# Rotating the banded attention's tensors in halves, with shorter pauses, in a two-layer hybrid backbone kernel

## The chip, the cores and the metric

The kernel runs on one core of one Trainium2 chip. The metric is the device time of one execution in microseconds, taken as the median of several runs. The engines are TensorE (PE; its weight loads are PEld), VectorE (DVE), ScalarE (ACT), GpSimd (POOL) and SyncE (SP), which issues nearly all DMA transfers.

## What is computed

The reference is a backbone of two layers over 1024 latent tokens and 256 context tokens, 1024 wide, in f32. Each layer splits one input projection among three kinds of heads, concatenates what they give, projects it back, and ends with a gated MLP:

```python
qa, kva, kr, z, xbc, dtr, swq, swk, swv = split_cols(h @ p['w_in'], IN_SPLITS)
...
qa_l = mla_queries(qa, p['mla_q_norm_g'], p['mla_w_uq'], pos)      # rotated by position
y_a = mla_latent_attention(qa_l, ka, va, ka_c, va_c)               # A: 6 heads, dense
...
yb, _ = ssd_bidirectional(xs, bm, cm, dt, a, h_ctx, True)          # B: scan, both directions
y_b = ssd_output(yb, xs, z, p['ssm_d'], p['ssm_norm_g'])
...
qs = axial_rope(swq.reshape(b, s, SWA_HEADS, SWA_HEAD_DIM), *pos) * scale
ks = axial_rope(swk.reshape(b, s, SWA_KV_HEADS, SWA_HEAD_DIM), *pos)
y_c = swa_latent_attention(qs, ks, vs, ks_c, vs_c, p['swa_sink'])  # C: banded, 4 heads
x = x + g1 * (jnp.concatenate([y_a, y_b, y_c], axis=-1) @ p['w_out'])
x = x + g2 * conv_glu(h2, p['ffn_w_up'], p['ffn_conv_w'], p['ffn_conv_b'], p['ffn_w_down'])
```

`axial_rope` is the rotation that the change is about: each tensor is multiplied by a cosine table, a copy of it with pairs exchanged is multiplied by a sine table, and the two are added. The first layer updates the context tokens too, the second does not.

## The kernel before

Tokens lie along the free axis, channels along the partitions, so a row tile is 128 x 1280 (1024 latent columns, then 256 context columns; `LAT` and `CTXS` in the code). A product in full precision is three matmuls on a high and a low part of each operand (`qh`, `ql`, `kh`, `kl`; `mixh`, `mixl`; `wh`, `wl`): the high part is a ScalarE copy to fp32r, the low part a VectorE subtraction.

In the middle of each layer the dense latent attention (A) is the foreground. Head after head it walks over ten key tiles; for each there are scores (`s<-qh,kh` and its two low products), an exponential on ScalarE (L1442), an addition to the sum of exponentials (`acc`, L1449, on GpSimd or VectorE), and matmuls with the values (`py<-P,vt`). The maxima of the next head (`pm`, `px`, reduced on VectorE at L1358 and L1349, then `mr` L1364 and the transposition `pr`) are made meanwhile.

In the background of that, one generator, `side()`, runs first the scan (B, function `ssd`), then the banded attention (C, function `swa`). The foreground keeps a modelled time, `self.t`, which only its and the background's matmuls advance. At each of its calls of `tick()` the background is let go one step further if the time that it asked for has come; a `yield p` asks for a pause of `p` modelled microseconds. The pauses stand in the table `PACE`, with one number for each layer. So the text of the program, and with it the order on TensorE, is set when the kernel is written out. On ScalarE and VectorE a background instruction is held behind the foreground instruction that was written ahead of it.

The last steps of the scan's generator are, for each chunk, the outputs (`main`), the pause `sq`, and `tail`: the sum of squares `py<-ones,z` on TensorE, whose input z is an ACT product (L998) behind VectorE's L994 and L996. Then `swa` begins. It loads its tensors from DRAM (`swr`, L1046), rotates the keys and the two halves of the queries one after the other (`rotate`, L788 to L793: shuffle, times sine, times cosine, addition, each 128 x 1024), splits them (copy L1049, subtraction L1050), writes both parts to DRAM (L1052) and pauses for `rot`. After the pause `sw0` come its own maxima (`sx`, `sb`, `sr`) and then units of work: scores `s<-qq,kk`, exponentials, additions to `acc` (L1176 to L1179), values, and at the end `pd`, a reciprocal (L1195) and the product `yc` (L1196). The first layer has six units, the second four.

When `swa` is done, its pool is closed, a new pool is opened in that memory, and the first two weights of the output projection (`w_out`) are loaded into it (`wload`, L413; split by L423 and L424). Another stage reads `w_out`'s other operand, `mixh` and `mixl`, the split of the concatenated heads (L798, L799). The projection's first matmuls are `p<-mixh,w`.

Of the kernel before, what the change touches and what calls it, by code (L numbers as in the profile page):

```python
# [20 lines left out]
SEQ = 1024  # L21
# [26 lines left out]
CTXS = slice(SEQ, NT)  # L48
# [11 lines left out]
def _rope_tables():  # L60
# [23 lines left out]
PACE = {  # L84
    'dt': (22.0, 22.0),
    'back0': (4.0, 4.0),
    'back': (3.0, 3.0),
    'cb': (0.5, 0.5),
    'exp': (0.5, 0.5),
    'ce': (0.5, 0.5),  # L90
    'fwd0': (4.0, 4.0),
    'fwd1': (5.0, 5.0),
    'sq': (2.0, 2.0),
    'next': (1.5, 1.5),
    'rot': (3.0, 3.0),
    'sw0': (14.0, 14.0),
    'swm0': (1.0, 1.0),
    'swa': (1.0, 1.0),
    'swb': (1.0, 1.0),
    'swv': (1.0, 1.0),  # L100
    'swx': (1.0, 1.0),
    'swe': (6.0, 6.0),
    'qpe': (6.0, 6.0),
    'mx1': (1.5, 1.5),
    'mx2': (1.5, 1.5),
    'mx3': (1.5, 1.5),
# [8 lines left out]
class Emit:  # L115
# [672 lines left out]
    def rotate(self, t, sh, cos, sin, rows, mask):  # L788
# [3 lines left out]
        nc.vector.tensor_mul(t[:rows, LAT], t[:rows, LAT], cos[:rows, LAT])  # L792
        nc.vector.tensor_add(t[:rows, LAT], t[:rows, LAT], sh[:rows, LAT])  # L793

    def split(self, src, rows, n, name, pool=False):
        nc = self.nc
        h, lo = self.u(F32R, name=name + "h"), self.u(F32R, name=name + "l")
        nc.scalar.copy(h[:rows, :n], src[:rows, :n])  # L798
        (nc.gpsimd if pool else nc.vector).tensor_sub(lo[:rows, :n], src[:rows, :n], h[:rows, :n])  # L799
        return h, lo  # L800


    def ssd(self, l, krdt, out):
        nc, c = self.nc, l == 0
# [87 lines left out]
        order = [9, 8] + list(range(7, 0, -1))  # L892
# [16 lines left out]
        order = [8, 9] + list(range(8))  # L909
        st = {}  # L910

        def load(k):
            s = st[k] = {"tm": load_tm(k)}
            if not (c or k < 8):
                return
            s["fm"] = M.tile([128, 7, 128], F32, tag="fm", name=self.nm("fm"))
            nc.sync.dma_start(out=s["fm"], in_=self.fmd[k])
            s["ab"] = []
            for d in range(2):
                ab = M.tile([128, SH, 128], F32, tag="ab", name=self.nm("ab"))  # L920
                nc.sync.dma_start(out=ab, in_=self.acsd[d * 6:d * 6 + 6, k, :].unsqueeze(0).to_broadcast([128, SH, 128]))
                s["ab"].append(ab)
            s["hb"] = None
            if k != 9:
                s["hb"] = M.tile([128, 384], F32, tag="hb", name=self.nm("hb"))
                nc.sync.dma_start(out=s["hb"], in_=self.hbd[k])
            s["z"] = M.tile([128, 3, 128], F32, tag="z", name=self.nm("z"))
            nc.sync.dma_start(out=s["z"], in_=self.zd[k])
# [72 lines left out]
        def tail(k):  # L1001

            s = st.pop(k)
            if "py" not in s:
                return
            for i in range(3):
                self.mm(out=s["py"][:, 384:385], lhsT=s["z"][:, i, :], rhs=self.ones[:, 0:1], start=(i == 0), stop=(i == 2))
            nc.vector.tensor_copy(vst[:, k:k + 1], s["py"][:, 384:385])
# [9 lines left out]
        for i, k in enumerate(order):  # L1018
            hf = main(k, hf)
            if i + 1 < len(order):  # L1020
                yield from prep(order[i + 1])
            yield PACE['sq'][l]
            tail(k)
            if i + 2 < len(order):
                load(order[i + 2])
            yield PACE['next'][l]
        n = NCH if c else 8
# [4 lines left out]
    def swa(self, l, Y):  # L1032
        nc, c = self.nc, l == 0
        sm = self.small[l]
        mask = [i ^ 16 for i in range(32)]
# [4 lines left out]
        cos, sin = self.u(name="cos"), self.u(name="sin")  # L1040
        nc.sync.dma_start(out=cos[:, LAT], in_=self.I['rope'][2])
        nc.sync.dma_start(out=sin[:, LAT], in_=self.I['rope'][3])
        for i in (0, 2, 3):
            n = NT if i == 0 else nq
            t, sh = self.u(name="swr"), self.u(name="sh")
            nc.sync.dma_start(out=t[:, 0:n], in_=self.swd[i][:, 0:n])  # L1046
            self.rotate(t, sh, cos, sin, 128, mask)
            h = [M.tile([128, NT], F32R, tag="k", name=self.nm(x)) for x in ("swh", "swl")]
            nc.scalar.copy(h[0][:, 0:n], t[:, 0:n])  # L1049
            nc.vector.tensor_sub(h[1][:, 0:n], t[:, 0:n], h[0][:, 0:n])  # L1050
            for p in range(2):
                nc.sync.dma_start(out=self.shd[i][p][:, 0:n], in_=h[p][:, 0:n].bitcast(F32))  # L1052
            yield PACE['rot'][l]
        vr, vt = self.u(name="swv"), self.u(name="vt")
        nc.sync.dma_start(out=vr, in_=self.swd[1])
        yc = [self.u(name="yc") for _ in range(2)]
# [71 lines left out]
        for u, (kv, s0, e0) in enumerate(units):  # L1128
# [19 lines left out]
            for i, (k, c0, c1) in enumerate(todo):  # L1148
                n = c1 - c0
# [51 lines left out]
    def mla_proj(self, l, kva, qn, kbuf, qh, load, maxes):  # L1201

        nc, c = self.nc, l == 0
# [20 lines left out]

        def rotated(t):

            self.rotate(t, self.u(name="sh"), cos, sin, 128, mask)
            yield PACE['qpe'][l]
            qp = self.split(t, 128, nq, "qp")
            for p in range(2):  # L1230
                nc.sync.dma_start(out=self.qpd[1][p][:, 0:nq], in_=qp[p][:, 0:nq].bitcast(F32))
# [37 lines left out]
        mask = [i ^ 8 for i in range(32)]  # L1269
        cos, sin = self.u(name="cos"), self.u(name="sin")  # L1270
# [29 lines left out]
        t = self.u(name="qpe")  # L1300
        small(wq, qn, 448, 128, some, self.evac(t, 128))
        self.bg(rotated(t), 1.0)
        values(range(2, 4))
        key(1)
# [932 lines left out]
```

## Time and profile before

| what | value |
|---|---|
| median of three runs | 3254.55 us (3251.92 to 3255.03) |
| the profiled execution | 3257.76 us |
| its span in the trace | 3255.6 us |
| granted TensorE clock, mean over the span | 0.965 |
| TensorE busy | 3057.9 us, 94% |
| VectorE busy | 2126.9 us, 65% |
| ScalarE busy | 1273.0 us, 39% |
| attention stage, first layer | about 400 to 788 us |
| attention stage, second layer | about 2080 to 2458 us |

The clock is given as a share of full speed. Its two levels are 1.2 and 2.4 GHz, so that a stretch with a mean of 0.65 was partly at the lower one. A wait of TensorE counts directly, as it is busy for 94% of the span; waits of the other engines count only where TensorE waits for them.

### The profile page before, as it was taken

What the parts mean: (1) busy time and instruction counts of PE and PEld (TensorE: products, weight loads), DVE (VectorE), ACT (ScalarE), POOL (GpSimd) and SP (SyncE); (2) the same over time, 40 slices, a digit from 0 to 9 for tenths busy, and PEclk for the clock granted to TensorE, in tenths of its full rate; (3) what the DMA queues carried; (4) which work ended last, traced back from release to release, by engine and by line L of the source; (5) the groups of instructions that cost most, each with busy time, mean ns of one, the idle gap of its engine ahead of it and who ended that gap; (6) DMA issues with size and microseconds to landing.
All of it is one profiled execution on the core that took longest, in us unless ns stands there. A gap on an engine that the chain in (4) does not pass through costs nothing.

```text
span 3255.6 us, 40074 instructions
## 1 busy us (share of the span) xinstructions
PE 3057.9 (94%) x15369; PEld 2404.6 (74%) x15369; DVE 2126.9 (65%) x3250; ACT 1273.0 (39%) x2204; POOL 421.0 (13%) x259
## 2 busy tenths in 40 slices
PE   6989978998999999998999999888999999999998
PEld 4778754554878888887888788754557778888887
DVE  4785787776285566668865635887563667677544
ACT  5334543443263343343111543543342444444212
POOL 2101113543100000000001200123452000000001
PEclk8999988999999999999999999988999999999999
DMA  8665676102312212227543345754113122225321
GB/s 269 217 194 152 215 223 168 39 16 86 106 41 67 78 56 72 78 67 287 179 149 104 122 112 169 236 168 131 42 35 115 52 78 80 89 84 180 131 75 62
DMA packets 349247, 392.41 MB, mean 121 GB/s; under 512 B 37202, under 2 KB 276451, under 8 KB 349056
## 3 DMA queue, kind: packets, MB, share of 16 engines
q1 hardware_dynamic: 348092, 389.62, 37.9%
q8 instruction: 121, 1.98, 0.3%
q0 software_dynamic: 704, 0.14, 0.1%
q14 instruction: 70, 0.57, 0.1%
q10 hardware_dynamic: 260, 0.10, 0.0%
HBM read 284.48 MB, written 104.01 MB: 119 GB/s over the span
## 4 chain that ended last, share of the span: by engine, by line
PE 80%; DVE 13%; ACT 2%; issue 2%; DMA 2%; POOL 0%; SPq 0%; DVEq 0%; ACTq 0%; POOLq 0%
PE p L143 36%; PE X L143 10%; PE Z L143 7%; PE s L143 5%; PE py L143 5%; PE pc L143 4%; PE V L143 3%; PE Y L143 3%; DVE mx L1358 1%; PE pm L143 1%; PE pn L143 1%; DVE wm L354 1%; PE pst L143 1%; DMA xr<-in_x_dram 1%; DVE acc L1393 1%
## 5 line engine op out<-in xcount | busy, mean ns | idle before, releaser
L143 PE MATMUL p<-gh,wb 128*128 128x512 f32 (+1 forms) x1760 | 504.9, 371 | 0.0
L436 ACT CAST wb<-w 128x512 fp32r<-128x512 f32 (+1 forms) x412 | 251.5, 613 | 597.4 <-PE p L143 304.4
L437 DVE TENSOR_TENSOR wb<-w,wb 128x512 fp32r<-128x512 f32 (+1 forms) x412 | 279.1, 679 | 239.4 <-ACT wb L436 237.9
L143 PEld LDWEIGHTS p<-gh,wb 128*128 128x128 f32 x1760 | 321.1, 189 | 56.0 <-issue 0.2
L1568 DVE SCALAR_TENSOR_TENSOR x<-p,modT,x 128x512 f32<-128x512 f32 (+1 forms) x280 | 193.0, 694 | 249.2 <-PE p L143 248.8
L143 PE MATMUL X<-hb,wb 128*128 128x512 f32 x1440 | 340.4, 389 | 1.6 <-DVE cm L1606 1.6
L143 PE MATMUL p<-gl,wb 128*128 128x512 f32 (+1 forms) x880 | 325.3, 370 | 0.3 <-DVE gl L1747 0.3
L143 PEld LDWEIGHTS X<-hb,wb 128*128 128x128 f32 x1440 | 270.1, 188 | 58.5 <-DVE cm L1606 2.5
L143 PE MATMUL p<-hhi,wh 128*128 128x512 f32 (+1 forms) x792 | 292.7, 377 | 5.5 <-ACT z L643 3.3
L143 PE MATMUL p<-hlo,wh 128*128 128x512 f32 (+3 forms) x792 | 290.8, 368 | 1.4 <-POOL hlo L2139 0.9
L143 PE MATMUL p<-hhi,wl 128*128 128x512 f32 (+1 forms) x744 | 272.7, 367 | 2.3 <-DVE wl L424 2.3
L1442 ACT ACTIVATE P<-s 128x512 f32<-128x512 f32 x240 | 142.3, 598 | 240.7 <-PE s L143 236.0
L143 PE MATMUL Z<-hb,wb 128*128 128x512 f32 x960 | 233.0, 392 | 3.6 <-ACT cm L1608 3.6
L143 PEld LDWEIGHTS Z<-hb,wb 128*128 128x128 f32 x960 | 179.9, 189 | 41.1 <-ACT cm L1608 4.4
L1449 POOL TENSOR_TENSOR acc<-acc,P 128x1024 f32<-128x1024 f32 x69 | 168.7, 2446 | 234.4 <-ACT P L1442 200.8
L143 PEld LDWEIGHTS p<-gl,wb 128*128 128x128 f32 x880 | 166.8, 190 | 28.4 <-DVE gl L1747 0.8
L143 PEld LDWEIGHTS p<-hhi,wh 128*128 128x128 f32 x792 | 152.6, 194 | 34.6 <-issue 4.4
L143 PE MATMUL py<-P,vt 128*64 128x512 f32 (+3 forms) x744 | 175.5, 588 | 0.2 <-DVE mx L1358 0.2
L143 PEld LDWEIGHTS p<-hlo,wh 128*128 128x128 f32 (+1 forms) x792 | 150.3, 190 | 24.6 <-DVE hlo L2133 1.5
L2085 POOL TENSOR_TENSOR acc<-acc,sq 128x512 f32<-128x512 f32 x24 | 32.0, 1339 | 1021.4 <-ACT sq L2084 1021.4
L143 PEld LDWEIGHTS p<-hhi,wl 128*128 128x128 f32 x744 | 142.8, 192 | 26.4 <-DVE wl L424 3.2
L354 DVE SCALAR_TENSOR_TENSOR wm<-wm,mstat,wm 128x512 f32<-128x512 f32 x196 | 141.1, 745 | 23.4 <-DMA wm<-in_w_mod_dram 22.8
(404 smaller groups left out, 5794.8 us busy)
## 6 DMA issues: line engine op xcount, KB each, us to landing
wm<-in_w_mod_dram SPq DMA_DIRECT2D x96, 512.0 KB
w<-in_ffn_w_up_dram SPq DMA_DIRECT2D x88, 512.0 KB
w<-in_ffn_w_down_dram SPq DMA_DIRECT2D x32, 512.0 KB
w<-in_w_in_dram SPq DMA_DIRECT2D x30, 512.0 KB
gd<-ft SPq DMA_DIRECT2D x22, 640.0 KB
gr<-gd SPq DMA_DIRECT2D x22, 640.0 KB
ab<-acsd SPq DMA_DIRECT2D x36, 384.0 KB
tm<-tmd SPq DMA_DIRECT2D x38, 320.0 KB
```

The source lines that it names most:

```text
L143: self.nc.tensor.matmul(out=out, lhsT=lhsT, rhs=rhs, start=start, stop=stop, **kw)
L354: nc.vector.scalar_tensor_tensor(out=acc[:, v, :], in0=w[:, i, :], scalar=c, in1=acc[:, v, :], op0=ALU.mult, op1=ALU.add)
L436: self.nc.scalar.copy(t[:, 0], raw)
L437: self.nc.vector.tensor_sub(t[:, 1], raw, t[:, 0])
L1358: nc.vector.tensor_reduce(out=m[:, j, s:s + 1], in_=p, axis=AXX, op=ALU.max)
L1393: nc.vector.reciprocal(rc, pd)
L1442: nc.scalar.activation(P[:, q * 512:(q + 1) * 512], s, AF.Exp, scale=sc)
L1449: (nc.vector if kt in ((2, 4, 6, 8) if self.scan else (4, 7)) else nc.gpsimd).tensor_add(acc, acc, P)
L1568: self.nc.vector.scalar_tensor_tensor(out=t[:, s:e], in0=p[:, 0:e - s], scalar=self.mcol(l, v, m)[:, o:o + 1], in1=t[:, s:e], op0=ALU.mult ...
L2085: (nc.gpsimd if self.n[ch] < 6 else nc.vector).tensor_add(acc, acc, sq[:, :n])
```

## The change

The three rotations in `swa` go by halves of 512 columns, and each operation is a step of the generator of its own, with a pause of 0.7 behind it (1.4 behind the addition and the copy); the subtraction of a half follows that pause. The 256 context columns are split in a step of their own. The rotation of the latent queries in `mla_proj` goes by halves too, with two pauses of 0.7 in each. `sw0` falls from 14 to 10 and `qpe` from 6 to 4. The pause `sq` of the last chunk of the scan grows by 4.

```diff
-    'rot': (3.0, 3.0),
-    'sw0': (14.0, 14.0),
+    'rot': (0.7, 0.7),
+    'sw0': (10.0, 10.0),
...
-    'qpe': (6.0, 6.0),
+    'qpe': (4.0, 4.0),
...
+    def rotate_steps(self, t, sh, cos, sin, rows, mask, hi, lo, n, pause):
+
+        nc, v = self.nc, self.nc.vector
+        for a in (0, 512):
+            r = slice(a, a + 512)
+            v.stream_shuffle(sh[rows, r], t[rows, r], mask)
+            yield pause
+            v.tensor_mul(sh[rows, r], sh[rows, r], sin[rows, r])
+            yield pause
+            v.tensor_mul(t[rows, r], t[rows, r], cos[rows, r])
+            yield pause
+            v.tensor_add(t[rows, r], t[rows, r], sh[rows, r])
+            nc.scalar.copy(hi[rows, r], t[rows, r])
+            yield 2 * pause
+            v.tensor_sub(lo[rows, r], t[rows, r], hi[rows, r])
+            yield pause
+        if n > SEQ:
+            nc.scalar.copy(hi[rows, CTXS], t[rows, CTXS])
+            yield pause
+            v.tensor_sub(lo[rows, CTXS], t[rows, CTXS], hi[rows, CTXS])
...
-            yield PACE['sq'][l]
+            yield PACE['sq'][l] + (4.0 if i + 1 == len(order) else 0.0)
             tail(k)
...
-            self.rotate(t, sh, cos, sin, 128, mask)
             h = [M.tile([128, NT], F32R, tag="k", name=self.nm(x)) for x in ("swh", "swl")]
-            nc.scalar.copy(h[0][:, 0:n], t[:, 0:n])
-            nc.vector.tensor_sub(h[1][:, 0:n], t[:, 0:n], h[0][:, 0:n])
+            yield from self.rotate_steps(t, sh, cos, sin, slice(0, 128), mask, *h, n, PACE['rot'][l])
             for p in range(2):
                 nc.sync.dma_start(out=self.shd[i][p][:, 0:n], in_=h[p][:, 0:n].bitcast(F32))
-            yield PACE['rot'][l]
...
-            self.rotate(t, self.u(name="sh"), cos, sin, 128, mask)
+            sh = self.u(name="sh")
+            for a in (0, 512):
+                r = slice(a, a + 512)
+                nc.vector.stream_shuffle(sh[:, r], t[:, r], mask)
+                nc.vector.tensor_mul(sh[:, r], sh[:, r], sin[:, r])
+                yield 0.7
+                nc.vector.tensor_mul(t[:, r], t[:, r], cos[:, r])
+                nc.vector.tensor_add(t[:, r], t[:, r], sh[:, r])
+                yield 0.7
             yield PACE['qpe'][l]
```

Three places show what moves. The first is the end of the scan on TensorE, first layer: outputs of the last chunk (`py<-ab,hf` and the like), then the squares `py<-ones,z`, between foreground scores. Before:

```order
L143 MATMUL py_4185<-ab_4033,hb_4035 64x128 x2
L143 MATMUL py_4185<-L_4083,tm_4027 64x128 x2
L143 MATMUL pm_4212<-kh_3781,qh_3785 128x512
L143 MATMUL py_4185<-ones,z_4037 128x1 x3
L143 MATMUL s_4232<-qh_3343,kh_3339 128x512
L143 MATMUL s_4232<-ql_3344,kh_3339 128x512
L143 MATMUL s_4232<-qh_3343,kl_3340 128x512
```

Now:

```order
L143 MATMUL s_4240<-qh_3343,kl_3340 128x512
L143 MATMUL px_4248<-kh_3779,qh_3783 128x256 x2
L143 MATMUL py_4116<-P_4117,vt_3540 64x512 x2
L143 MATMUL py_4116<-P_4146,vt_3540 64x512 x2
L143 MATMUL pm_4257<-kh_3779,qh_3783 128x512
L143 MATMUL s_4261<-qh_3343,kh_3339 128x512
L143 MATMUL s_4261<-ql_3344,kh_3339 128x512
L143 MATMUL s_4261<-qh_3343,kl_3340 128x512
L143 MATMUL pm_4266<-kh_3779,qh_3783 128x512
L143 MATMUL py_4189<-ones,z_4041 128x1 x3
L143 MATMUL s_4273<-qh_3343,kh_3339 128x512
```

The squares now stand 15 rows later, behind three groups of foreground scores, two rows of values and four maxima: 9,216 columns in all. In the second layer they stand 7 rows later, four of them values.

The second place is VectorE behind the end of the scan, first layer: `swr`, `sh` and `swl` are the rotation, `mx<-pm` and `mx<-px` the foreground's maxima. Before:

```order
L1358 TENSOR_REDUCE mx_4246<-pm_4289 128x1
L1358 TENSOR_REDUCE mx_4246<-pm_4297 128x1
L793 TENSOR_TENSOR swr_4262<-swr_4262,sh_4263 128x1024
L790 STREAM_SHUFFLE sh_4301<-swr_4300 128x1024
L1449 TENSOR_TENSOR acc_4111<-acc_4111,P_4283 128x1024
L1358 TENSOR_REDUCE mx_4246<-pm_4314 128x1
L1349 TENSOR_REDUCE mx_4246<-px_4329 128x2
L1358 TENSOR_REDUCE mx_4246<-pm_4338 128x1
L791 TENSOR_TENSOR sh_4301<-sh_4301,sin_4259 128x1024
L792 TENSOR_TENSOR swr_4300<-swr_4300,cos_4258 128x1024
L1050 TENSOR_TENSOR swl_4270<-swr_4262,swh_4269 128x1280
```

Now:

```order
L1475 TENSOR_TENSOR acc_4115<-acc_4115,P_4260 128x1024
L399 RECIPROCAL vst_460<-vst_460 128x10
L1375 TENSOR_REDUCE mx_4246<-px_4313 128x2
L802 TENSOR_TENSOR sh_4302<-sh_4302,sin_4298 128x512
L1384 TENSOR_REDUCE mx_4246<-pm_4323 128x1
L804 TENSOR_TENSOR swr_4301<-swr_4301,cos_4297 128x512
L1384 TENSOR_REDUCE mx_4246<-pm_4332 128x1
L1384 TENSOR_REDUCE mx_4246<-pm_4343 128x1
L806 TENSOR_TENSOR swr_4301<-swr_4301,sh_4302 128x512
L1384 TENSOR_REDUCE mx_4246<-pm_4351 128x1
L1375 TENSOR_REDUCE mx_4357<-px_4359 128x2
L1390 TENSOR_REDUCE mr_4247<-mx_4246 128x4
```

Before, whole operations of 1024 columns, two of them and a subtraction of 1280 in a row, stand between two maxima; in these rows there is now one operation of 512 between two maxima. Further on, where the maxima of a head are done, three or four halves stand together.

The third place is TensorE at the end of the attention stage, first layer: `s<-qh,kh` are scores of the foreground (here those of the context tokens), `s<-qq,kk` scores of the banded attention, `p<-mixh,w` the output projection. Before, the banded attention's last sum (`pd<-acc_6489`) is 20 rows ahead of the projection, and foreground work stands between:

```order
L143 MATMUL s_6584<-qh_5528,kh_5524 128x256
L143 MATMUL s_6584<-ql_5529,kh_5524 128x256
L143 MATMUL s_6584<-qh_5528,kl_5525 128x256
L143 MATMUL py_6373<-P_6551,vt_3542 64x512 x2
L143 MATMUL py_6373<-P_6568,vt_3542 64x512 x2
L143 MATMUL py_6597<-P_6585,vt_3542 64x256
L143 MATMUL py_6597<-P_6585,ones 64x256
L143 MATMUL py_6597<-P_6585,vt_3542 64x256
L143 MATMUL py_6597<-P_6585,ones 64x256
L143 MATMUL p_6644<-mixh_6352,w_6610 128x512
```

Now:

```order
L143 MATMUL s_6608<-qq_6449,kk_5823 128x256
L143 MATMUL s_6608<-q_1232_6450,k_1086_5824 128x256
L143 MATMUL s_6608<-qq_6449,kk_5823 128x256
L143 MATMUL s_6608<-q_1232_6450,k_1086_5824 128x256
L143 MATMUL s_6615<-qq_6449,kk_5823 128x256
L143 MATMUL s_6615<-q_1232_6450,k_1086_5824 128x256
L143 MATMUL s_6615<-qq_6449,kk_5823 128x256
L143 MATMUL s_6615<-q_1232_6450,k_1086_5824 128x256
L143 MATMUL py_6604<-P_6607,vt_4805 64x256 x2
L143 MATMUL py_6604<-P_6614,vt_4805 64x256 x2
L143 MATMUL pd_6627<-acc_6603,ones 64x256 x2
L143 MATMUL p_6672<-mixh_6091,w_6638 128x512
```

Now the last unit of the banded attention and the one ahead of it stand alone behind the foreground's last score: 18 of the layer's 64 banded score tiles, 88 matmuls with 25,600 columns in all between that score and the projection. In the second layer it is 10 of 56 tiles, 58 matmuls with 17,408 columns. Before, in both layers, no banded score stands behind it; the projection follows 8 matmuls of the foreground's values. The order of SP moves with it: the load of the projection's first weight is issued behind that last banded score, as before.

## Rows read from the trace of the kernel before

**Rows 1.** The page, parts 1 and 5: busy time of the engines, two groups.

```profile
PE 3057.9 (94%) x15369; PEld 2404.6 (74%) x15369; DVE 2126.9 (65%) x3250; ACT 1273.0 (39%) x2204; POOL 421.0 (13%) x259
...
L1449 POOL TENSOR_TENSOR acc<-acc,P 128x1024 f32<-128x1024 f32 x69 | 168.7, 2446 | 234.4 <-ACT P L1442 200.8
```

**Rows 2.** Waits of TensorE, first layer, 460 to 800 us.

```profile
PE pd L143 <- DVE acc L1179: 10.7, 3, 9.4
PE pr L143 <- DVE mr L1364: 6.9, 4, 4.8
PE s L143 <- DVE mx L1358: 6.1, 3, 4.9
PE py L143 <- ACT z L998: 4.3, 1, 4.3
PE p L143 <- DVE w L424: 4.0, 1, 4.0
```

**Rows 3.** Timeline of TensorE, second layer: the last squares, in brackets idle and releaser.

```profile
2181.81 1.44 PE L143 MATMUL py<-ones,z 128*128 128x1 f32 x6 [4.32 <-ACT z L998]
```

**Rows 4.** Windows: PE, PEld, DVE, ACT, POOL busy (instructions), granted clock, DMA.

```profile
400.00:450.00 50.00, 41.07 (x238) 32.89 (x236) 45.58 (x88) 29.21 (x84) 5.62 (x5) 0.85 0.90 286
470.00:480.00 10.00, 7.47 (x23) 4.45 (x23) 5.72 (x14) 4.29 (x6) 2.37 (x1) 0.66 0.46 151
490.00:500.00 10.00, 2.55 (x7) 1.13 (x5) 10.00 (x10) 1.19 (x2) 3.33 (x1) 0.68 0.45 158
500.00:510.00 10.00, 7.23 (x26) 3.72 (x27) 9.41 (x11) 4.88 (x7) 0.00 (x0) 0.64 0.85 264
790.00:800.00 10.00, 7.25 (x25) 5.83 (x26) 7.70 (x7) 4.20 (x4) 0.00 (x0) 0.83 1.06 351
2180.00:2190.00 10.00, 8.19 (x29) 4.11 (x30) 4.19 (x6) 5.14 (x6) 2.36 (x1) 0.67 0.18 64
2190.00:2200.00 10.00, 7.17 (x28) 4.52 (x27) 9.37 (x11) 3.59 (x6) 4.88 (x2) 1.00 1.02 279
2200.00:2210.00 10.00, 8.81 (x25) 4.01 (x24) 10.00 (x12) 2.71 (x4) 3.02 (x2) 0.66 0.48 146
2210.00:2220.00 10.00, 6.08 (x18) 4.19 (x19) 9.93 (x12) 2.94 (x5) 0.00 (x0) 0.69 0.81 256
2220.00:2230.00 10.00, 10.00 (x38) 4.27 (x36) 5.33 (x9) 2.99 (x5) 4.96 (x2) 0.80 1.02 314
```

**Rows 5.** Timeline of VectorE, first layer: start, duration, instruction.

```profile
489.06 1.90 DVE L791 TENSOR_TENSOR sh<-sh,sin 128x1024 f32<-128x1024 f32 x1
...
492.01 3.62 DVE L1050 TENSOR_TENSOR swl<-swr,swh 128x1280 fp32r<-128x1280 f32 x1
```

**Rows 6.** Timeline of VectorE, second layer.

```profile
2194.38 2.95 DVE L791 TENSOR_TENSOR sh<-sh,sin 128x1024 f32<-128x1024 f32 x1
```

**Rows 7.** Groups by shape, 560 to 780 us: busy us, mean ns, idle before.

```profile
L1195 DVE RECIPROCAL acc<-pd 128x512 f32<-128x512 f32 x4 | 13.4, 3358 | 5.5 <-PE pd L143 5.5
L1196 DVE TENSOR_TENSOR yc<-py,acc 128x512 f32<-128x512 f32 x4 | 2.7, 683 | 0.0
...
L1442 ACT ACTIVATE P<-s 128x512 f32<-128x512 f32 x79 | 46.9, 600 | 77.6 <-PE s L143 74.9 <-DVE mx L1358 1.3 <-DVE acc L1393 0.4
```

**Rows 8.** Timeline of TensorE: last banded score, last-but-one values.

```profile
775.38 0.28 PE L143 MATMUL s<-q,k 65*128 65x256 f32 x1
...
782.52 1.94 PE L143 MATMUL py<-P,vt 128*64 128x512 f32 x8
```

**Rows 9.** Timeline of the DMA queue SP, 765 to 800 us.

```profile
775.57 15.81 SPq L413 DMA_DIRECT2D w<-in_w_out_dram  x5
```

**Rows 10.** Window of 1 us: DMA share and GB/s are the last columns.

```profile
778.00:779.00 1.00, 1.00 (x7) 0.49 (x3) 0.97 (x3) 0.00 (x0) 0.00 (x0) 1.00 0.69 207
```

**Rows 11.** Timelines of ScalarE and VectorE: first output weight, high and low part.

```profile
786.03 1.04 ACT L423 CAST w<-w 128x1024 fp32r<-128x1024 f32 x1
...
791.47 1.23 DVE L424 TENSOR_TENSOR w<-w,w 128x1024 fp32r<-128x1024 f32 x1
```

## The prediction

> **What bounds the kernel now.** I read the page first: TensorE is busy for 94% of the span, VectorE for 65% [rows 1]. So time is lost where TensorE waits or where its clock is low. Next come its waits in the two attention stages. In the first layer four are near the change: squares waiting for z, 4.3 us; `pr` and `s` waiting for the foreground's maxima on VectorE, 6.9 and 6.1 us; `pd` for the banded sum, 9.4 us; and 4.0 us for the first output weight [rows 2]. The second layer has the same wait for z, 4.32 us [rows 3]. The table of windows adds what a list of waits hides. From 490 to 500 us VectorE is busy for all of 10.00 us while TensorE does 2.55 us; and where TensorE has waited, the clock granted to it falls: 0.66 at 470 to 480, 0.64 at 500 to 510, against 1.00 at 2190 to 2200 [rows 4]. What does VectorE do there? A sine product of 1.90 us and a subtraction of 3.62 us stand in it, in front of a maximum that TensorE needs [rows 5]. So the rotations are on the path, by way of VectorE's order.
>
> **The change, term by term.** The sum is made against the profiled run's own 3257.76 us, which is 3.2 above the median of the runs; differences are then put on the median, 3254.55.
>
> A, the longer pause ahead of the last squares. In the first layer 9,216 columns of foreground matmuls now come ahead of them. Eight matmuls of 512 columns took 1.94 us [rows 8], 0.24 each, so that is 18 x 0.24 = 4.3 us, against a wait of 4.3 [rows 2]; the second layer's seven rows come to about as much against 4.32 [rows 3]. The waits give 8.6 us. The windows around them had the clock at 0.66 with 7.47 us busy and 0.67 with 8.19 [rows 4]; at full clock that work takes 0.34 x 7.47 + 0.33 x 8.19 = 5.2 us less. At most -13.8, at least 0 if another wait ends at the same place. Three maxima and a sum of 1024 columns still stand on VectorE there, so I keep a little back: -12.
>
> B, the rotations by halves. Before, the idle time of TensorE beside them is 7.45 us (490 to 500) and 2.77 (500 to 510), 10.2 together; in the second layer 2.83 + 1.19 + 3.92 = 7.9 (2190 to 2220) [rows 4]. The low clock costs 0.32 x 2.55 + 0.36 x 7.23 = 3.4, and 0.34 x 8.81 + 0.31 x 6.08 + 0.20 x 10.00 = 6.9 (2200 to 2230). That is 28.4 us at stake. The order shows a half between two maxima where whole tensors and a subtraction of 1280 stood. A half is 0.68 us, by the nearest row of that shape [rows 7], so a maximum is now late by one of these and no more by 1.90, 1.2 and 3.62 in a row. But the total on VectorE doesn't fall: two halves are 1.37 us against 1.23 for a whole [rows 11], about 1 us more for each tensor, six tensors. It is covered, as TensorE has more foreground work there (some 67 us of matmuls by the same price, between the squares and the first `sx` in the first layer's order) than VectorE has operations in the same stretch (some 49 us, priced by rows 5 and 7); without that cover it is 6 us. And some of the waits are for scan normalisation and reciprocals, which stay. Bounds: -28 if all goes, -6 if only what the two longest rows exceed their plain length gives way (3.62 less 1.5, which is 1.23 x 1.25, and 2.95 less 1.2, and the clock of such waits). The order argues for more than half: two thirds, -19.
>
> C, the latent queries by halves and `qpe` at 4. From 400 to 450 us VectorE is busy for 45.58 of 50 us [rows 4], so breaking up gains no time of its own and the added instructions may cost; TensorE's 41.07 leaves room on both sides. 0, between -3 and +3. The Trainium skill ("Perfetto Trace Analysis", section "Optimizing Scalar/DVE Operations") says that each operation has a fixed overhead, some 60 ns on VectorE, so grouping pays on a saturated engine, whereas breaking up helps where an engine isn't saturated but makes others wait. It speaks against the change here and for it in B; by an estimate from its 60 ns, C would be about +1 and the sum would hardly move.
>
> D, the stall of 9.4 us ahead of `pd` [rows 2]. VectorE is there held up by the splitting of the mixed heads at the last head's start. That block stays where it is and meets the banded attention at an earlier unit: in the new order a transposition of its maxima (`sr`) stands behind three `mixl` on VectorE. Some 7 us of the 9.4 come back there: -2, bounds -9 and +1.
>
> E, the first layer's uncovered end. Since `swa` now asks for its own time at many more steps, it is later in spite of the smaller `sw0`: 18 score tiles stand alone at the end. Their matmuls have to run anyway (25,600 columns, 12 us). What is added is waiting, worked out step by step down the order. (1) `sr` behind one `mixl` and the last maxima on VectorE: 1.5. (2) `pd` of the big unit behind its last exponential and addition, 0.60 + 0.68 [rows 7], less 0.5 of values: 0.8. (3) `pd` of the last unit needs a sum whose second addition stands on VectorE behind the reciprocal: 3.36 + 0.68 + 0.68 + 0.68 [rows 7] = 5.4, less 1.4 of scores and values: 4.0. (4) the projection's third matmul needs the low part of the weight, behind another reciprocal of half the columns: 3.36 / 2 + 1.23 [rows 11], less two matmuls: 2.4. The weight itself is no later: its request went out at 775.57, right behind the last banded score at 775.38 [rows 8, 9], its data were nearly all in by 779 [rows 10], and the cast takes 1.04 [rows 11], together some 5 us beside (3) and (4). Sum 8.7. In such a stretch the clock falls as in rows 4: 0.35 of some 14 us of work is 5. It replaces 4.0 us of waiting [rows 2] and 0.17 x 7.25 = 1.2 of clock (790 to 800) [rows 4]. 8.7 + 5 - 5.2 = +8.5, bounds +3 (no fall of the clock) and +22 (below).
>
> F, the second layer's end. No wait for the weight stood there before. 10 tiles, 17,408 columns, 8.2 us of work. `pd` waits 1.3 for the last addition, and the third matmul for a reciprocal and a low part, 3.36 + 1.23 less 0.5: 4.1; with small waits for exponentials, 5.9, and 2 for the clock: +8, bounds +3 and +19.
>
> Sum: -12 - 19 + 0 - 2 + 8.5 + 8 = -16.5. On the own run 3241.3, on the median 3238.
>
> **Rivals.**
> 1. Slower, through the two ends. There nothing lies beside the banded work, so scores, exponential and addition of each tile may go in single file, at the lower clock throughout. First layer: 8.7 + 12 (the clock) + 11 exponentials at 0.6 = 27.3, less 5.2: +22. Second layer: 5.9 + 8.2 + 9 x 0.6 = +19. Then -33 + 41 = +8: 3263. For it: the banded sum alone makes TensorE wait 9.4 us before [rows 2]. Against it: two score buffers of a tile let TensorE run ahead. It decides once the ends cost over 33 + 6.5 us together.
> 2. The ends take the gain, half-way to that: +30 together, about -3: 3251, no change.
> 3. Halves don't free VectorE, since it waits for GpSimd: a sine product took 2.95 us in the second layer and a subtraction 3.62 in the first where 1024 columns plainly take 1.23 [rows 5, 6, 11], and an addition on GpSimd lasts 2.45 [rows 1]. A half that meets one is as late as a whole. Then B gives 6: 3254.55 - 3.5 = 3251, and the change doesn't do what it is to do. The Trainium skill ("SBUF — State Buffer", section "SBUF: two separate sides") says that the port shared by the two is an exclusive lock for a whole instruction. The trace's long rows agree with that; how often a half meets one, it can't show.
> 4. More comes back: B whole, -28, and D whole, -9: -12 - 28 - 9 + 16.5 = -33: 3222. For it: the new order has nowhere more than a few halves in a row.
>
> **Numbers.** A measurement of this kernel tells 0.2%, 6.5 us, from no change. My forecast (3228 to 3248) 0.40, more gain 0.16, ends eat it 0.13, GpSimd 0.13, slower 0.18. Faster by over 0.2% is the first two, 0.56; within it 0.26; slower 0.18. The range of 8 in 10 reaches from 3222 (rival 4) to 3262, near rival 1; the outermost tenth on either side is left out.
>
> **What the new profile would show.** A right: no wait of `py<-ones,z` over 1 us at either scan's end. B right: no window of 10 us with TensorE under 7 us in the 40 us behind it, and the clock near 1. D right: a wait of some 7 us at `sr`. E and F right: behind the foreground's last score 9 and 6 us of idle TensorE, in steps (3) and (4) above all, and a clock near 0.65. The prediction is wrong if the ends are longer than 22 us of loss in a layer, or if VectorE's halves last over 1.5 us each.

## The result: 0.9% slower

The changed kernel takes 3281.05 us in the median (3280.06 to 3283.91) against 3254.56 before. The ratio is 1.009 (1.0078 to 1.0102). The forecast was 3238 (3222 to 3262) and faster: wrong by sign, and 19 us above the range. Its profiled run has a span of 3278.4 us, 22.8 more than before.

TensorE's waits after the change, first layer (460 to 830 us; total, times, longest), answer to [rows 2]:

```profile
PE sr L143 <- DVE smr L1134: 15.1, 3, 12.4
PE pr L143 <- DVE mr L1390: 7.5, 3, 3.3
PE pr L143 <- DVE smr L1134: 2.8, 1, 2.8
```

And in the second layer (2170 to 2500 us):

```profile
PE pn L143 <- DVE dg L403: 5.6, 1, 5.6
PE p L143 <- DVE w L424: 3.4, 1, 3.4
```

The waits for z are gone from the top, and so is the old 9.4 ahead of `pd`; a wait of 12.4 us ahead of `sr` is new. To see where the time went I cut both layers' attention stages at five rows that both programs have: the foreground's first score, the last squares, the first banded maxima `sx`, the foreground's last score, and the projection's first matmul. What TensorE loses in a stretch is its idle time plus (1 - clock) x busy. After, by stretch (four for each layer; columns as in [rows 4]):

```profile
452.64:468.51 15.87, 14.94 (x97) 10.55 (x94) 15.32 (x27) 7.01 (x14) 5.16 (x2) 1.00 0.25 98
468.51:563.75 95.24, 80.28 (x335) 44.88 (x335) 77.26 (x118) 36.68 (x64) 35.20 (x14) 0.91 0.57 166
563.75:774.19 210.44, 181.80 (x906) 104.01 (x907) 131.00 (x168) 82.32 (x142) 92.65 (x42) 0.92 0.08 21
774.19:804.02 29.83, 24.51 (x122) 12.21 (x120) 21.52 (x22) 14.55 (x24) 0.00 (x0) 0.81 0.18 50
2151.14:2193.40 42.26, 38.67 (x226) 25.09 (x225) 35.29 (x51) 22.30 (x49) 14.75 (x7) 0.96 0.34 103
2193.40:2289.86 96.46, 78.67 (x295) 42.42 (x293) 78.82 (x101) 32.90 (x56) 34.62 (x14) 0.86 0.49 140
2289.86:2457.80 167.94, 155.49 (x741) 89.43 (x742) 113.61 (x140) 71.11 (x123) 76.73 (x35) 0.92 0.08 20
2457.80:2475.99 18.19, 15.32 (x84) 6.61 (x83) 6.58 (x4) 9.37 (x14) 13.82 (x7) 0.99 0.52 145
```

Before, the second and third stretch of each layer:

```profile
472.53:525.02 52.49, 41.21 (x164) 23.18 (x164) 41.55 (x51) 20.53 (x31) 15.10 (x6) 0.80 0.64 206
525.02:785.09 260.07, 237.93 (x1201) 136.92 (x1202) 185.48 (x232) 108.58 (x190) 116.80 (x52) 0.96 0.16 38
2181.81:2235.04 53.23, 45.29 (x157) 24.75 (x158) 40.02 (x48) 20.33 (x31) 17.84 (x8) 0.80 0.76 221
2235.04:2454.09 219.05, 203.93 (x963) 115.33 (x962) 138.81 (x177) 91.79 (x156) 101.34 (x47) 0.93 0.15 41
```

The banded attention is late: `sx` comes 95 us behind the squares instead of 52. So more foreground work lies in the second stretch and less in the third, and the two are best read together. First layer: 11.3 + 0.20 x 41.2 and 22.1 + 0.04 x 237.9 give 51 us lost before; 15.0 + 0.09 x 80.3 and 28.6 + 0.08 x 181.8 give 65 after. Second layer: 46 before, 54 after. The uncovered end adds 5.3 + 0.19 x 24.5 = 10 and 3. Ahead of the squares 3.7 and 6 are won. That is +14 + 8 + 10 + 3 - 10 = 25. In its first 25 us the second layer's projection loses 6 more and the first layer's 1 less. So the stages lose 30 us more, and the spans differ by 22.8, as some 6 come back ahead of the first stretch.

Those 6 belong to the one run: before's profile reaches the first foreground score at 458.14 us, and every later kernel, some with nothing changed ahead of it, at 450 to 455.

### The profile page after: what moved, and what is told of

It reads as the page before. It is cut to its first block, busy times and chain, and to the rows that moved or that the text cites. A ratio compares the mean times of both kernels' runs of the same rounds, so it can differ in the third digit from the quotient of the medians.

```text
span 3278.4 us, 40136 instructions
## 1 busy us (share of the span) xinstructions
PE 3068.0 (94%) x15369; PEld 2402.9 (73%) x15369; DVE 2150.6 (66%) x3300; ACT 1273.3 (39%) x2214; POOL 417.5 (13%) x259
## 4 chain that ended last, share of the span: by engine, by line
PE 78%; DVE 14%; DMA 2%; ACT 2%; issue 2%; POOL 1%; SPq 0%; DVEq 0%; ACTq 0%; POOLq 0%
PE p L143 36%; PE X L143 10%; PE Z L143 7%; PE s L143 5%; PE py L143 5%; PE pc L143 4%; PE V L143 3%; PE Y L143 3%; DVE mx L1384 2%; PE pm L143 1%; DVE wm L354 1%; PE pn L143 1%; DMA xr<-in_x_dram 1%; PE pst L143 1%; DVE acc L1419 1%
## 5 line engine op out<-in xcount | busy, mean ns | idle before, releaser
L143 PEld LDWEIGHTS Z<-hb,wb 128*128 128x128 f32 x960 | 179.8, 189 | 41.2 <-ACT cm L1634 4.6
L354 DVE SCALAR_TENSOR_TENSOR wm<-wm,mstat,wm 128x512 f32<-128x512 f32 x196 | 141.0, 746 | 22.6 <-DMA wm<-in_w_mod_dram 22.0
```

What stands on the lines that cost most here:

```text
L143: self.nc.tensor.matmul(out=out, lhsT=lhsT, rhs=rhs, start=start, stop=stop, **kw)
L354: nc.vector.scalar_tensor_tensor(out=acc[:, v, :], in0=w[:, i, :], scalar=c, in1=acc[:, v, :], op0=ALU.mult, op1=ALU.add)
```

## The experiments

Ratios are to the kernel before, which each experiment ran again beside its own kernel (medians from 3251.2 to 3252.3 us), in brackets their 95% interval. They aren't quotients of the medians and can differ from those by 0.1%. 1 us is 0.00031.

**One part at a time.** Lateness alone; the pause ahead of the squares alone; the latent queries alone; all of the change at the old place. e_late is the kernel before with

```diff
-    'sw0': (14.0, 14.0),
+    'sw0': (48.0, 44.0),
```

> The kernel before with nothing of the change in it but lateness: the pause sw0 is 48 and 44 instead of 14, so that the banded attention's first maxima and the number of its score tiles left behind the foreground's last score (18 and 10) are those of the changed kernel. Theory 1 (lateness is the whole loss: the banded work meets the heads' mixing in the first layer, is pressed into fewer foreground heads, and stands alone at the end): by the stretches of the two traces the loss is 12 + 6 + 8 us in the first layer and 4 + 8 in the second, 38 together, so about 3290 us (3280 to 3300). Rival (the two uncovered ends are what lateness costs, 8.5 + 8, the rest is the halves' added instructions): about 3271 us (3264 to 3276).

Measured: 3259.27 us, 1.002 (1.001 to 1.0029). Neither theory: lateness costs 7 us, not 38 and not 17. But its `sx` stands eight matmuls of TensorE ahead of the changed kernel's, which the part on the place below shows to matter.

e_sq is the kernel before with

```diff
-            yield PACE['sq'][l]
+            yield PACE['sq'][l] + (4.0 if i + 1 == len(order) else 0.0)
```

> The kernel before with only the longer pause ahead of the scan's last squares. Theory 1: the two waits for z go (4.3 each in the profile of before), 9 us with a little of the clock: 3245 us (3241 to 3249). Rival: another wait of VectorE's ends at the same place, as its order is otherwise the same: 3254 us (3250 to 3258).

Measured: 3252.15 us, 1.0001 (0.999 to 1.0011). The rival. Its trace (TensorE, first layer) has no wait for z over 1 us, but has these:

```profile
483.08 0.59 PE L143 MATMUL pr<-identr,mr 128*1 128x128 f32 x4 [6.53 <-DVE mr L1364]
...
516.69 0.77 PE L143 MATMUL sx<-kk,qq 128*128 128x256 f32 x2 [6.86 <-DMA qq<-shd]
```

The wait for maxima was 4.84 there before, and the banded queries now arrive 6.9 us late for their maxima, for which nothing waited before.

e_qpe takes only the latent queries' part of the diff, with `qpe` 4.

> The kernel before with only the latent queries' rotation by halves and the pause qpe at 4. Theory 1: the 3 us by which the changed kernel reached the first layer's first foreground score sooner are this: 3251 us (3248 to 3254). Rival: VectorE is full there and has more instructions: 3256 us (3254 to 3260).

Measured: 3252.46 us, 1.0003 (0.9994 to 1.0012): no effect, as term C had it.

e_halves is the changed kernel with

```diff
-    'rot': (0.7, 0.7),
-    'sw0': (10.0, 10.0),
+    'rot': (0.0, 0.0),
+    'sw0': (18.0, 18.0),
```

> The changed kernel with the pauses in the banded attention's rotation at 0 and sw0 at 18, so that its first maxima stand where they stand when only the pause ahead of the last squares is made longer; no score tile is left behind the foreground's last score. The halves, the longer pause and the latent queries by halves are all in it. Theory 1: the halves lose nothing and win some 2 to 10 us beyond the 12 of the other two parts: 3238 us (3230 to 3244). Rival (halves cost): over 3246 us.

Measured: 3258.65 us, 1.0026 (1.0014 to 1.0039). The kernel loses some 8 us where the halves were to win. Theory 1 falls, and the parts don't add up: 0.2% and 0.26% alone, 0.9% together.

**The block of splits.** In the changed kernel's first layer VectorE (L820), GpSimd (L820) and TensorE stand like this around 720 us:

```profile
715.53 1.49 DVE L820 TENSOR_TENSOR mixl<-yb,mixh 128x1280 fp32r<-128x1280 f32 x1 [1.19 <-ACT mixh L819]
720.04 3.79 DVE L820 TENSOR_TENSOR mixl<-yb,mixh 128x1280 fp32r<-128x1280 f32 x1 [3.01 <-ACT mixh L819]
723.76 4.16 DVE L820 TENSOR_TENSOR mixl<-ya,mixh 128x1280 fp32r<-128x1280 f32 x1
719.60 2.88 POOL L820 TENSOR_TENSOR mixl<-yb,mixh 128x1280 fp32r<-128x1280 f32 x1
722.45 4.12 POOL L820 TENSOR_TENSOR mixl<-ya,mixh 128x1280 fp32r<-128x1280 f32 x1
728.41 0.58 PE L143 MATMUL sr<-identr,smr 128*1 128x128 f32 x4 [12.43 <-DVE smr L1134]
```

The three `mixl` of VectorE stand ahead of the two small operations that `sr` needs. Two of them last 3.8 and 4.2 us, where the first took 1.49 for the same shape; GpSimd is making its own two at that time. In between VectorE waits 3.0 us for ScalarE's high part (`mixh`). Two kernels spread these splits, a_spread in the changed kernel and b_spread in the one before:

```diff
                 for i in (3, 4, 5, 0, 1):
                     self.mix(l, Y, i, hl, i in (4, 1))
+                    yield
...
-            if h == NH - 1:
-                last()
+            mixes = last() if h == NH - 1 else iter(())
+            next(mixes, None)
...
+                if kt % 2:
+                    next(mixes, None)
```

> The changed kernel, but the five splits of the mixed heads at the start of the last foreground head go one by one, at its start and at its key tiles 1, 3, 5 and 7, instead of all at once; the order on TensorE is the same row for row. Theory 2 (what makes the changed kernel slower than lateness alone is that in the first layer the maxima of the banded attention run into this block: sr waits 12.4 us behind two splits of 3.8 and 4.2 us, and the clock falls after it): 12 us of waiting and some 4 of clock go, about 3264 us (3258 to 3270). Rival (the block only moves, or the loss is spread over small waits on VectorE): 3274 us or more.

Measured: 3270.46 us, 1.006 (1.0048 to 1.0073): against the changed kernel 0.3%, 10 us of the 16.

> The kernel before with the same spreading of the five splits and nothing else. Theory 2: the wait of 9.4 us ahead of pd goes with the 1.8 us of clock behind it, 3241 us (3238 to 3247). Rival (the block only moves): 3252 us.

Measured: 3258.03 us, 1.0013 (1.0005 to 1.0022). In its trace the wait ahead of `pd` is 4.5 instead of 9.4, yet the kernel is not faster. The trace shows where most of it goes: at the start of the second layer's projection, where a reciprocal (L1393) stands on VectorE behind the split of a weight. TensorE's longest wait there, before and in b_spread (2.1 in e_qpe, 0.8 in e_sq):

```profile
2471.62 0.50 PE L143 MATMUL p<-mixh,w 128*128 128x512 f32 x1 [1.88 <-DVE acc L1393]
2468.11 0.79 PE L143 MATMUL p<-mixh,w 128*128 128x512 f32 x1 [5.91 <-DVE acc L1393]
```

That is 4.0 us more, with 2.6 of clock behind it, in place of the 4.9. A wait that is shorter in one trace isn't a gain in time.

b_best is b_spread with e_sq's edit and `sw0` at 18 and 14.

> The kernel before with the longer pause ahead of the last squares, the splits of the mixed heads spread, and sw0 at 18 and 14, so that the banded queries have landed when their maxima begin (with only the longer pause, these waited 6.9 us for the load in the first layer). Theory 2: 9 us from the squares, 10 from the splits, 3233 us (3228 to 3242). Rival (a part of each only moves to the next wait on VectorE): 3243 us or more.

Measured: 3255.28 us, 1.0008 (0.9998 to 1.0018): the rival. The same wait is 6.1 us here.

**Halves against steps.** e_whole puts the old whole rotations, one step for each tensor, within four rows of the changed kernel's place: it is the kernel before with the edits of e_sq and e_qpe and

```diff
-    'sw0': (14.0, 14.0),
+    'sw0': (48.0, 40.0),
```

> The changed kernel with whole rotations in the banded attention: the old rotation, copy and subtraction in one step for each tensor, rot at 3 and sw0 at 48 and 40, so that the first maxima stand within four rows of those of the changed kernel and as many score tiles (18 and 10) are left behind. Longer pause ahead of the last squares and latent queries by halves are in it. If the halves gain what the prediction gave them, it is 15 to 20 us slower than the changed kernel, 3297 us. Theory 2 (halves gain next to nothing, the collision of the late maxima with the splitting of the heads is the loss): within 6 us of the changed kernel if the maxima meet the block in the same way, and some 15 us faster, 3262 us, if the few rows by which they differ keep sr away from it.

Measured: 3244.39 us, 0.9974 (0.9965 to 0.9983). It is faster than before and than every forecast for it, with the same 18 and 10 tiles uncovered. Its second to fourth stretches:

```profile
466.99:556.80 89.81, 79.53 (x330) 44.89 (x330) 73.14 (x95) 35.59 (x57) 36.90 (x14) 0.90 0.62 176
556.80:750.39 193.59, 178.13 (x910) 103.15 (x911) 129.10 (x170) 82.53 (x143) 94.11 (x42) 0.96 0.08 22
750.39:780.66 30.27, 24.54 (x122) 12.03 (x120) 18.14 (x21) 14.54 (x24) 0.66 (x1) 0.82 0.19 53
2171.53:2256.85 85.32, 77.22 (x295) 42.79 (x293) 66.85 (x82) 32.60 (x52) 34.50 (x14) 0.86 0.65 178
2256.85:2422.49 165.64, 154.62 (x742) 89.17 (x743) 114.96 (x140) 71.13 (x123) 76.73 (x35) 0.93 0.04 10
2422.49:2440.53 18.04, 15.16 (x84) 6.60 (x82) 6.83 (x4) 9.25 (x14) 13.81 (x7) 1.00 0.51 146
```

Against the changed kernel the end is the same, 5.7 + 0.18 x 24.5 = 10.1. The first layer's third stretch loses 15.5 + 0.04 x 178.1 = 22.6 instead of 43, the second layer's second 8.1 + 0.14 x 77.2 = 19 instead of 29. 30 of the 37 us between the two profiles are in these two. Three kernels take halves and steps apart. h_one is e_whole with the halves in one step (the first part of the diff). w_steps is the changed kernel with whole operations, `rot` 1.5 and `sw0` 13 and 14 (the second). a_scan is the changed kernel with the flag that divides the foreground's sums falling behind the rotations (the third):

```diff
-            self.rotate(t, sh, cos, sin, 128, mask)
+            for a, e in ((0, 512), (512, 1024)):
+                r = slice(a, e)
+                nc.vector.stream_shuffle(sh[:, r], t[:, r], mask)
...
-        for a in (0, 512):
-            r = slice(a, a + 512)
+        for a in (0,):
+            r = slice(a, a + 1024)
...
-                self.scan = False
                 self.bg(self.scan_norm(l, Y, out["vst"]), PACE['sn0'][l])
...
+        self.scan = False
         vr, vt = self.u(name="swv"), self.u(name="vt")
```

> As the late kernel with whole rotations (pauses, places and 18 and 10 tiles behind the same), but each rotation by halves of 512 in one step, all operations of a tensor one behind the other. Theory 3 (halves as such cost: 15 of 48 two-input halves in the changed kernel met an addition on GpSimd and took 1.4 to 2.1 us instead of 0.68, against 6 of 24 whole operations there): 8 us above the late kernel with whole rotations, 3252 us (3249 to 3260). Theory 4 (the steps cost, not the halves: single operations drawn out over 95 us stand in front of every chain of VectorE, and set where the maxima meet the splits): as the late kernel with whole rotations, 3244 us (3240 to 3248).

Measured: 3247.16 us, 0.9987 (0.9978 to 0.9997), in theory 4's range: halves as such cost some 4 us, 0.13%, if anything, for the two intervals overlap.

> The changed kernel with whole operations of 1024 columns instead of halves, still one step and one pause for each operation (pause 1.5, sw0 at 13 and 14, which puts the banded maxima within ten rows of the changed kernel's and leaves 18 and 10 tiles behind). Theory 3: near the late kernel with whole rotations, 3247 us (3242 to 3254). Theory 4: near the changed kernel, 3275 us (3268 to 3285).

Measured: 3258.62 us, 1.0021 (1.0011 to 1.0031): steps as such cost 0.47%, some 15 us, between the theories. Its `sx` stands four matmuls ahead of e_whole's; from `sr` on the order is the same. TensorE loses 26 and 25 us between the squares and `sx` where e_whole loses 18 and 19:

```profile
468.12:565.65 97.53, 82.83 (x326) 45.82 (x326) 75.27 (x95) 35.06 (x59) 37.05 (x14) 0.86 0.55 162
2180.13:2274.22 94.09, 81.08 (x295) 43.43 (x293) 72.39 (x83) 32.80 (x53) 36.20 (x14) 0.85 0.60 162
```

> The changed kernel, but while the rotations run the foreground's sums stay divided as during the scan: four additions in ten on VectorE instead of two, so that GpSimd has five of 2.35 us for each head instead of seven. The order on TensorE is the same row for row. Theory 3: fewer halves meet one, 6 to 10 us less, 3273 us (3270 to 3277). Theory 4: VectorE has more to do in the same stretch, 3281 us or more.

Measured: 3277.32 us, 1.0083 (1.007 to 1.0097): within the interval of the changed kernel, and between the theories. Fewer halves meet an addition on GpSimd (8 are stretched instead of 13), but VectorE has these additions to do itself, and the time is the same.

w_early is e_whole with `sw0` at 36 and 30.

> The late kernel with whole rotations at sw0 36 and 30 instead of 48 and 40: 5 score tiles are left behind the foreground's last score in the first layer and none in the second. If the uncovered ends cost what the trace says (10 us ahead of the projection in the first layer, 3 ahead of it and 5 behind in the second), most of it goes: 3234 us (3228 to 3240). Rival (in the first layer the banded sum meets the splits of the heads again, as in the kernel before, and the second layer's wait for the weight only changes its place): 3246 us or more.

Measured: 3243.4 us, 0.9977 (0.9968 to 0.9986). Nearer the rival: nothing won against e_whole. In the second layer no banded score is left at the end, but `pd` of the last unit now waits for the sum on GpSimd, in place of the end:

```profile
2442.47 1.12 PE L143 MATMUL pd<-acc,ones 128*64 128x512 f32 x2 [6.48 <-POOL acc L1179]
```

**The place.** The kernels whose first `sx` of the first layer stood at TensorE's row 1984 had the 12.4 us (but for the spread splits), those at 1976 or 1980 had not. One number moves it. x_nine is the changed kernel, x_49 is e_whole, each with one of these:

```diff
-    'sw0': (10.0, 10.0),
+    'sw0': (9.0, 10.0),
...
-    'sw0': (48.0, 40.0),
+    'sw0': (49.0, 40.0),
```

> The changed kernel with one number changed: sw0 of the first layer is 9 instead of 10. The first banded maxima stand four rows of TensorE sooner, and from there the order of the banded rows snaps to that of the late kernel with whole rotations (sr at the same rows). Theory 5 (some 18 us of the changed kernel's loss is this place: sr behind the splits of the heads 12.4 us, pr behind the banded maxima 2.8 and 3.3, and the clock after them): 3260 us (3256 to 3266). Rival (the loss belongs to the halves and steps and is only moved): 3275 us or more.

> The late kernel with whole rotations with one number changed: sw0 of the first layer is 49 instead of 48, which puts its banded maxima and sr at the rows of the changed kernel in the first layer, without halves or steps. Theory 5: the same 18 us are lost, 3262 us (3257 to 3267). Rival (the halves and steps are needed for the loss): 3246 us.

Measured: x_nine 3265.12 us, 1.0038 (1.0026 to 1.0051); x_49 3270.87 us, 1.0048 (1.0036 to 1.006). Against the changed kernel x_nine wins 0.5%, 17 us; against e_whole x_49 loses 0.7%, some 24. x_49 loses more than was forecast. The wait follows the place, not the halves: x_49, without halves or steps in the banded rotations, differs from the changed kernel in TensorE's order by 14 of 15,369 matmuls, and the wait is the same. TensorE in x_49:

```profile
726.20 0.58 PE L143 MATMUL sr<-identr,smr 128*1 128x128 f32 x4 [12.43 <-DVE smr L1116]
```

and what stands in x_nine where the changed kernel has it:

```profile
722.83 0.79 PE L143 MATMUL s<-qq,kk 128*128 128x512 f32 x1 [2.82 <-DVE smx L1115]
```

x_nine settles more. TensorE's matmuls stand in the same order in x_nine, h_one and e_whole, all 15,369 of them, so the three differ in their banded rotations alone: halves in steps against whole ones 0.64%, 21 us; steps, halves in both, 0.5%, 17 us. The stretches of x_nine between the squares and `sx` lose 22 and 30 us, e_whole's 18 and 19:

```profile
469.82:563.82 94.00, 79.35 (x331) 44.11 (x331) 75.85 (x116) 36.09 (x63) 35.19 (x14) 0.91 0.57 167
2181.94:2280.58 98.64, 82.42 (x294) 44.19 (x292) 80.04 (x101) 32.92 (x56) 34.11 (x14) 0.83 0.48 137
```

So the way from the kernel before to the changed one is, by ratios: lateness +7 us (e_late), the longer pause and the latent queries -15 (e_whole), halves in steps +21 (x_nine), the place +17. That is 30 us, or 0.9%.

w_mix is e_whole with `sw0` at 36 and 40.

> The late kernel with whole rotations with the first layer's sw0 of 36 (5 tiles behind) and the second layer's of 40 (10 behind), each the better of the two by the stretches of the traces: from the first foreground score to the projection the first layer lost 50.6 us at 48 and 48.5 at 36, the second 50.4 at 40 and 60.0 at 30. Theory 5 (the places in the layers add up): 2 us below the late kernel, 3242 us (3238 to 3245). Rival: no difference from it that can be told, 3245 us or more.

Measured: 3243.71 us, 0.9977 (0.9968 to 0.9986), in theory 5's range but not to be told from e_whole or w_early, and like them 0.2 to 0.3% faster than before.

## Why the prediction was wrong

**A, -12: nothing when made alone, right in size with the late banded attention.** The step held as far as it went: the wait for z fell from 4.3 to 0.6 us in the first layer and left the second. The bound "0 if another wait ends at the same place" was named and set aside; e_sq shows it was right there: the maxima of the next head and the queries' loads were the next to be late. With the late banded attention the same edit, with C's, takes e_late's 1.002 to e_whole's 0.9974, 15 us. In the two profiles all of it lies ahead of `sx`: there e_late loses 59 us in both layers and e_whole 44, and from `sx` on to 25 us into the projection each loses 66, with `sr` at the same rows. So it is hardly a better place. e_qpe makes C nothing in the kernel before; beside the late banded attention C was not tried alone.

**B, -19: the step that failed.** With TensorE's order held the same the rotations in halves and steps lose 21 us instead (x_nine against e_whole). "So a maximum is now late by one of these and no more by 1.90, 1.2 and 3.62 in a row" counted what stands directly ahead of a maximum. It left out two things. First, steps draw the rotations out: w_steps has no halves there and loses 15 us against e_whole, in the stretch up to `sx`. Single operations now stand in front of other chains of VectorE, the scan's normalisation too: in the second layer `pn` waits for `dg`, 5.6 us in the changed kernel and x_nine and 3.5 in w_steps, but not in e_whole or h_one. Second, rival 3 was true in part. VectorE, GpSimd and TensorE of the changed kernel, second layer:

```profile
2228.16 2.02 DVE L802 TENSOR_TENSOR sh<-sh,sin 128x512 f32<-128x512 f32 x1
2230.11 0.68 DVE L804 TENSOR_TENSOR swr<-swr,cos 128x512 f32<-128x512 f32 x1
2231.84 0.68 DVE L806 TENSOR_TENSOR swr<-swr,sh 128x512 f32<-128x512 f32 x1
2233.23 2.19 DVE L802 TENSOR_TENSOR sh<-sh,sin 128x512 f32<-128x512 f32 x1
2235.34 3.36 DVE L403 TENSOR_TENSOR dg<-ident,vst 128x1024 f32<-128x1024 f32 x1
2227.26 2.37 POOL L1475 TENSOR_TENSOR acc<-acc,P 128x1024 f32<-128x1024 f32 x1 [2.67 <-ACT P L1468]
2232.51 5.10 POOL L1475 TENSOR_TENSOR acc<-acc,P 128x1024 f32<-128x1024 f32 x2 [2.88 <-ACT P L1468]
2238.75 2.08 PE L143 MATMUL pn<-dg,ones 128*128 128x512 f32 x2 [5.55 <-DVE dg L403]
```

Halves that meet no addition of GpSimd take 0.68 us, the two here that start while one runs 2.0 and 2.2, and `dg`, with two inputs as well, 3.36 instead of 1.21. Of the 24 two-input halves in a layer's rotations 7 (first) and 8 (second) met one, with means of 1.37 and 2.06; in e_whole 3 of 12 whole ones in each, at 2.3 and 2.5. That is 4.8 and 11 us of VectorE in a layer against 3 and 4. It comes with the steps more than with the halves: w_steps' whole operations lose 5 and 8 us so, the halves of h_one, in one step, 2 and 7. How much of the 17 to 21 us is this meeting, and how much the mere standing in front, no run separates.

**D, -2: 12.4 instead of 7.** The prediction saw `sr` behind three `mixl`, and put the wait there at some 7 us. They lasted 1.5, 3.8 and 4.2, VectorE waited 3.0 for a high part between them, and the clock was lost behind them. That this hangs on a single step of `sw0`, 10 or 9, it could not see from a price by halves and means; the order of the rows said it, had the place of `sr` been read against its neighbours a few rows on either side. It is worth some 17 to 24 us, with the 2.8 and 3.3 us of `pr` that come with it.

**E and F, +8.5 and +8: right in their sums.** First layer: 10 us lost ahead of the projection and 1.2 + 2.9 in its first 25 us, less the 5.5 that these had before, +8.6. The parts are partly luck: waiting is 6.5 us where the forecast had 8.7, the clock 7.5 where it had 5. Step (1) is there with 1.6 us, step (3) waits 0.6 instead of 4.0, and step (4), for the second reciprocal and the low part of the weight, 1.2 instead of 2.4. The first 25 us of the projection, after and before, in the first layer, then in the second:

```profile
804.02:829.02 25.00, 23.80 (x92) 17.89 (x93) 14.00 (x11) 4.44 (x4) 0.00 (x0) 0.88 0.63 216
788.03:813.03 25.00, 21.02 (x84) 15.78 (x83) 17.01 (x13) 6.72 (x7) 0.00 (x0) 0.93 0.72 237
2475.99:2500.99 25.00, 21.55 (x80) 15.94 (x79) 15.62 (x11) 3.04 (x3) 0.00 (x0) 0.80 0.42 147
2458.00:2483.00 25.00, 23.12 (x101) 17.93 (x100) 11.08 (x10) 4.90 (x6) 3.73 (x2) 1.00 0.39 107
```

Steps (3) and (4) are these:

```profile
802.38 1.12 PE L143 MATMUL pd<-acc,ones 128*64 128x256 f32 x4 [0.55 <-DVE acc L1195]
...
806.43 1.22 PE L143 MATMUL p<-mixh,w 128*128 128x512 f32 x2 [1.20 <-DVE w L424]
```

The clock too, in the window around it:

```profile
798.00:808.00 10.00, 6.62 (x22) 3.37 (x23) 9.87 (x9) 2.01 (x3) 0.00 (x0) 0.59 0.52 148
```

Second layer: 3 ahead, 6 more than before behind it (3.4 for the low part, and the clock), +9. But shortening them didn't give the time back: in w_early the second layer's `pd` waits 6.5 us instead, and the first layer loses 15.1 + 0.06 x 207 = 28 us in its third stretch, which holds more work, against e_whole's 23.

**C, 0:** right, 1.0003.

Rival 1 had the sign, by the wrong mechanism and 18 us short (3263): the ends cost what E and F said, not 41 us. What stays open: which part of the steps' cost is the meeting with GpSimd, and why A alone wins nothing, beyond the waits that e_sq's trace shows in its place.

## What to carry to other kernels

An operation that is cut in two and drawn out over time doesn't only hold others up for a shorter time: it stands ahead of other chains of its engine for longer, and each piece can meet the other engine's instructions anew. Where the order is written out by a modelled clock, time a neighbouring place or two of the moved work before pricing the edit: one step of one pause was worth 17 to 24 us here, as much as the whole gain that was forecast. And a wait that was taken away alone won nothing here (e_sq, b_spread): look for the waits that come next, by name, further on too.

## What the runs showed of the hardware

A half of 512 columns with two inputs lasts 0.68 us; of the 15 in the changed kernel that met an addition on GpSimd, 13 took 1.4 to 2.3. The 55 maxima that started during one in the same stretches, which have one input, and that in PSUM, kept their 0.68. The first half in the rows above ends 0.55 us after GpSimd's addition (2230.18 against 2229.63), as if it had waited for it. That agrees with the Trainium skill ("SBUF — State Buffer", section "SBUF: two separate sides"), by which the two engines' shared port is locked for a whole instruction. It was expected of the long rows of before; unexpected was that GpSimd and VectorE made the same kind of split side by side, and that VectorE's took 3.8 and 4.2 us instead of 1.5.
